# Depthwise convolution for two token tiles at once, as two half-rate streams with three short filters

## The chip, the cores and the metric

The kernel runs on one core of one Trainium2 chip. Its engines work side by side, each through its own queue of instructions in a fixed order: TensorE (PE in the profile; PEld is its weight load), VectorE (DVE), ScalarE (ACT), GpSimd (POOL) and SyncE (SP), which here only issues transfers. They meet through semaphores. Transfers are issued from the SP and ACT queues. The metric is the device time of one execution in microseconds; lower is better.

## The reference

One decoder layer in float32 on x of 2048 tokens by 1024 channels:

```
hn   = rms_norm(x);  proj = hn @ w_in                  # q, k, v and u (2 x 512 channels)
h    = a * sigmoid(gate)            # u = a, gate
h    = depthwise causal conv(h, width 31) + bias       # per channel, along the tokens
conv = silu(layer_norm(h over channels)) @ w_conv_pw
attn = sliding-window attention (window 128, sinks, relative bias)
h    = x + rms_norm(concat(attn, conv) @ w_out)
out  = h + rms_norm((silu(n @ w_gate) * (n @ w_up)) @ w_down),  n = rms_norm(h)
```

The part that changes is the depthwise convolution: y[n] is the sum over j from 0 to 30 of w[j] g[n - 30 + j], plus a bias, for 512 channels, each with its own 31 weights.

## The kernel before

The tokens are worked in four tiles of 512 (T), the channels in blocks of 128 partitions. Matmuls carry float32 as a high and a low part, three products for one (`three`). The stages, by the letter that the profile shows behind the @ of a tile's name:

- **A0 to A3** (`stage_a`): the input projections of one token tile, 14 units of 24 matmuls. The gated input of the convolution goes to DRAM, channel block by channel block (`glu`, stored in `glu_scr`, which sets `g{t}{c}` in `started`).
- **B0 to B3** (`stage_b`): attention, by blocks of 128 tokens. Its score bias lives in a tile of the tag `mb` until the last block.
- **C0 to C3**: the convolution, in two stages. `stage_taps(t)` loads one channel block with a halo of 30 tokens (`conv_in`, tag `glu`), makes the first product and then 30 multiply-and-add instructions on DVE, each over 512 tokens and each onto the accumulator y (tag `fc`), and stores y to `y_scr`. `stage_tail(t)` loads y again, turns it on TensorE, does the LayerNorm, the swish and the pointwise product, and stores the result to `mixT` (`conv_tail`). Its own work tiles have the tag `fc` too.
- **W0 to W3** (`stage_w`): the output projection of a token tile, which reads `mixT` (four attention blocks, then four blocks from the convolution), and its norm (`norm_w`).
- **H** (`stage_h_plain`, `stage_h_sums`), **F** and **G**: the channel mixer, for two pairs of token tiles, with seven products for eight. H turns the normed rows into operands; "S0" names the sums of operands for the first pair. F is the gate/up part: first plain products (`stage_pre`), then the sums with the other steps (`stage_p1`). G is the down part (`stage_p2`); in the first of them also the output projections of the second pair.

The order of work: the main line is a chain of `run(...)` calls; each of its steps moves a clock on by its cost. Beside it there are lanes (class `Lane`), lists of stages that give out work at a given rate per unit of that clock: `lc` the taps, `ld` the tails of tiles 0 and 1, `lw` the output projections, `lh` the operands, `lb` attention, and others. A stage in a lane can have a condition: W0 needs tail C0; C0 needs the taps T0 and ten units more; C3 likewise T3. From the code's emission order with priorities, a scheduler writes the fixed order of each queue. The taps are emitted with a priority 100 steps later than the main work (`LC`), and each is tied behind the last DVE instruction of the main work (`dve`). `BUFS` gives the number of buffers of each tag, which all tiles of this tag share.

The taps of tile 0 run during A0 and A1 and those of tile 1 behind them. During W1 and the first gate/up products the lane is held until S0 is done (`lc.hold`); tile 2's taps then go at a rate of 0.4 under the gate/up sums, tile 3's at 0.1 there and at 0.9 under the first down stage.

Of the kernel before, what the change touches and what calls it, by code (L numbers as in the profile page):

```python
# [12 lines left out]
F32 = mybir.dt.float32  # L13
F32R = mybir.dt.float32r
BF16 = mybir.dt.bfloat16
I8 = mybir.dt.int8
# [14 lines left out]
TAPS = 31  # L31
HALO = TAPS - 1
EPS = 1e-6
NEG = -1e30
# [3 lines left out]
def layer_kernel(ctx, tc, x, xT, cols, rows, sinks, relb, onehot, w_in, w_pw, w_out, w_gate, w_up, w_down, out):  # L38
# [13 lines left out]

    BUFS = dict(x=4, p=4, wx=1, gb=2, hl=8, ql=4, chl=5, mid=4, mb=2, fa=4, at=2, fc=3, glu=2, yt=1, raw=2, w=6)

# [6 lines left out]
    def f2(tag, shape=(P, T)):  # L61
        return t_(tag, shape)
# [161 lines left out]
    hn_scr = dr.tile([S, D], F32, name="hn_scr")  # L224
    y_scr = dr.tile([4, P, S], F32, name="y_scr")
    qs = {}
# [14 lines left out]
    def row_norms(ts, tag):  # L241
        lab[0] = f"A{ts[0]}"
        n = 4 * len(ts)
        ssq = sm(n)
        for i in range(n):
            xt = f4(tag)
            r0 = ts[0] * T + i * P
            nc.sync.dma_start(xt, x[r0 : r0 + P])
            act(junk, xt, AF.Square, accum_out=ssq[:, i : i + 1])
        r = rsqrt(ssq, n, D)  # L250
        for j, t in enumerate(ts):
            rn[t] = r[:, 4 * j : 4 * j + 4]
# [262 lines left out]

    def conv_in(t, c):
        g = t_("glu", (P, 576))[:, 0 : HALO + T]
        if t == 0:
            nc.vector.memset(g[:, 0:HALO], 0.0)
            nc.sync.dma_start(g[:, HALO:], glu_scr[c, :, 0:T])  # L520
        else:
            nc.sync.dma_start(g, glu_scr[c, :, t * T - HALO : (t + 1) * T])
        y = f2("fc")
        vts(y, g[:, 0:T], dwh[:, c, 0:1], dwb[:, c : c + 1], ALU.mult, ALU.add)
        return g, y

    def turner(yt, ycs):
# [7 lines left out]

    def stage_taps(t):
        L = f"C{t}"
        for c in range(4):
            while f"g{t}{c}" not in started:
                yield None  # L540
            lab[0] = L
            g, y = conv_in(t, c)
            for j in range(1, TAPS):
                stt(y, g[:, j : j + T], dwh[:, c, j : j + 1], y, ALU.mult, ALU.add)
                yield 0.68
                lab[0] = L
            nc.sync.dma_start(y_scr[c, :, t * T : (t + 1) * T], y)
            yield 0.68

    def stage_tail(t):  # L550
        L = f"C{t}"
        lab[0] = L
        yt = t_("yt", (P, 4, 4 * P))
        ycs = []
        turn = turner(yt, ycs)
        for c in range(4):
            lab[0] = L
            y = f2("fc")
            nc.sync.dma_start(y, y_scr[c, :, t * T : (t + 1) * T])
            ycs.append(y)  # L560
            turn(c)
            yield 0.5
        yield from conv_tail(t, yt)

    def conv_tail(t, yt):
# [30 lines left out]
        for m in range(4):  # L596
            raw = f2("fc")
            nc.sync.dma_start(raw, w_pw[m])
            w = split_w(raw, "mb" if t == 1 and m % 2 else "chl").rearrange("p a (k c) -> p a k c", c=P)
# [4 lines left out]
            nc.scalar.dma_start(mixT[4 + m, :, t * T : (t + 1) * T], z)  # L604
            yield 2
            lab[0] = L
# [102 lines left out]
    def norm_w(w, spill, acc, mtag):  # L709
# [4 lines left out]
        for s in range(4):  # L714
            act(junk, acc[s], AF.Square, accum_out=ssq[:, s : s + 1])
            yield 0.5
            lab[0] = L
# [4 lines left out]
        for s in range(4):  # L722
            lab[0] = L
            post_scale(acc[s], gb, r[:, s : s + 1])
            r0 = w * T + s * P
            if s == (2 if mtag == "fa" else 0):
                xt = f4("wx")
# [8 lines left out]
            nc.sync.dma_start(h_scr[r0 : r0 + P], acc[s])  # L736
            act(junk, acc[s], AF.Square, accum_out=ssq2[:, s : s + 1])
            yield 1.5
# [316 lines left out]
    def finish(L, gb, jobs, pool=True):  # L1055
# [3 lines left out]
        for j, (rows_, halves) in enumerate(jobs):  # L1059
            for n in range(2):  # L1060
                act(junk[:, 0:T], halves[n], AF.Square, scale=D**-0.5, accum_out=ssq[:, 2 * n + j : 2 * n + j + 1])
# [15 lines left out]
    def stage_p2(ws, am, td, last=False):  # L1077
# [60 lines left out]
        def scale_even(h):  # L1138
            for b in (2 * h, 2 * h + 1):
                lab[0] = L  # L1140
                c = home("c11", "x", b)
                act(junk[:, 0:T], c, AF.Square, scale=D**-0.5, accum_out=sse[:, b : b + 1])
                ptt(c, c, gbs[0], ALU.mult)
                yield 4.0

        def after(ty, b):
# [11 lines left out]
            elif ty == 3:  # L1158
                vtt(home("p7", "x", b), o, home("x2", "p", b), ALU.subtract)
                if b == 3:  # L1160
                    for n in range(2):
                        gbs.append(t_("glu", (P, 576))[:, 0:T])
                        nc.sync.dma_start(gbs[n], rows[1, n * T : (n + 1) * T].partition_broadcast(P))
# [48 lines left out]
        for b in range(4):  # L1212
# [3 lines left out]
            ssq = sm(1)  # L1216
            act(junk[:, 0:T], banks[b], AF.Square, scale=D**-0.5, accum_out=ssq)
            g = f2("fa")
# [59 lines left out]

    RC0, RC1, RC2, RC3, RW0, RW, RB, LC = 0.7, 1.1, 0.4, 0.9, 1.7, 1.25, 0.8, 100
    TAPS0 = 6  # L1280
# [6 lines left out]
    RT = 0.3  # L1287
    RP = 0.1
    NS = 12
# [171 lines left out]
```

## Time and profile before

| | us |
|---|---|
| median of 3 runs | 2048.06 |
| lowest and highest run | 2045.74, 2054.27 |
| profiled execution: span from first to last instruction | 2045.2 |
| TensorE busy | 1959.9 |
| DVE busy | 1499.2 |
| ACT busy | 984.4 |
| GpSimd busy | 408.5 |
| 480 tap instructions on DVE (the group's busy time) | 367.7 |

The profiled execution's own time is given as this span alone; no separate run time is listed for it, and the lowest run is 0.5 us above it. In a row that groups instructions one reads: line of the code, engine, operation, output tiles<-input tiles, shapes, xcount | busy us, mean ns of one | idle time of the engine before them and what ended it. DVE instructions issued through the helper `dve` all show its line, L85; they are told apart by tiles. A row of waits has: who waited <- for whom: us in total, times, longest. A row of a timeline has: start us, us, engine, line, operation, tiles, and in brackets the idle time before it and what ended it. A row of stages has the stretch, its length, and then the busy time and number of instructions of each engine in it.

### The profile page before, as it was taken

The page shows a single profiled execution, that of the slowest core. Times are in us where ns is not written, and L with a number is a line of the kernel's source. Part 1 is how long each engine was busy: PE and PEld are TensorE (multiplying, and loading weights), DVE is VectorE, ACT ScalarE, POOL GpSimd, SP SyncE. Part 2 cuts the span into 40 slices and gives each one's busy share as a digit, 9 for nine tenths or more (in the row PEclk, how much of TensorE's full clock was granted, in tenths as well). Part 3 has the DMA queues.
Part 4 walks back from the last instruction along what each step waited for, and adds up shares of the span by engine and source line. Part 5 has one row for each costly group of instructions (what it writes and reads, how often), then busy time and mean ns, then how long its engine had stood idle before and what let it go on. Part 6 is the DMA issues. An engine that isn't in the chain of part 4 may idle for free. (4 is left out here: it accounts for less than half of the span.)

```text
span 2045.2 us, 27190 instructions
## 1 busy us (share of the span) xinstructions
PE 1959.9 (96%) x8826; PEld 1565.3 (77%) x8826; DVE 1499.2 (73%) x2623; ACT 984.4 (48%) x1938; POOL 408.5 (20%) x466
## 2 busy tenths in 40 slices
PE   8999999999989999999989999999999999999997
PEld 6777767776667778778878878877788888888886
DVE  4999896995885899887749985577666665545557
ACT  5355455456546633334346457556643433345443
POOL 4011223333111300000001012115423333221003
PEclk9999999999999999999999999999999999999998
DMA  8787645578559876884486778678954453366654
GB/s 305 256 300 228 205 135 185 180 235 279 186 155 330 292 242 224 294 270 168 140 262 205 231 260 287 191 278 304 337 177 162 149 169 112 103 236 212 206 190 144
DMA packets 235902, 451.44 MB, mean 221 GB/s; under 512 B 23496, under 2 KB 49264, under 8 KB 235760
## 3 DMA queue, kind: packets, MB, share of 16 engines
q1 hardware_dynamic: 215216, 419.30, 62.6%
q10 hardware_dynamic: 20544, 30.42, 4.0%
q8 instruction: 69, 1.13, 0.2%
q14 instruction: 73, 0.60, 0.1%
HBM read 330.60 MB, written 119.02 MB: 220 GB/s over the span
## 5 line engine op out<-in xcount | busy, mean ns | idle before, releaser
L85 DVE SCALAR_TENSOR_TENSOR fc@C<-glu@C,colt,fc@C 128x512 f32<-128x512 f32 x480 | 367.7, 778 | 3.5
L846 PE MATMUL mm@F<-hl@H,w@F 128*128 128x512 f32 x1056 | 253.3, 390 | 2.5 <-ACT mm@F L886 1.5
L1116 PE MATMUL mm@G<-hl@G,hl@G 128*128 128x512 f32 x924 | 230.0, 398 | 8.2 <-DVE x@G L85 4.8
L846 PEld LDWEIGHTS mm@F<-hl@H,w@F 128*128 128x128 f32 x1056 | 197.6, 188 | 44.7 <-ACT mm@F L886 2.3
L170 PE MATMUL mm@A<-hl@A,w@A 128*128 128x512 f32 x840 | 207.3, 398 | 5.2 <-ACT w@A L110 1.4
L1116 PEld LDWEIGHTS mm@G<-hl@G,hl@G 128*128 128x128 f32 x924 | 174.6, 191 | 47.0 <-ACT hl@G L759 6.9
L1116 PE MATMUL mm@G<-w@G,hl@G 128*128 128x512 f32 x876 | 199.4, 389 | 0.0
L759 ACT ACTIVATE w@F<-chl@F 128x512 fp32r<-128x512 f32 x220 | 134.8, 624 | 130.9 <-PE mm@F L846 122.2
L1116 PEld LDWEIGHTS mm@G<-w@G,hl@G 128*128 128x128 f32 x876 | 164.4, 188 | 34.1
L170 PEld LDWEIGHTS mm@A<-hl@A,w@A 128*128 128x128 f32 x840 | 155.9, 189 | 42.2 <-ACT w@A L110 2.2
L85 DVE TENSOR_TENSOR w@F<-chl@F,w@F 128x512 fp32r<-128x512 f32 x198 | 145.4, 738 | 33.8 <-ACT w@F L759 33.4
L846 PE MATMUL mm@F<-ql@H,w@F 128*128 128x512 f32 x528 | 127.9, 391 | 11.0 <-ACT w@F L759 7.3
L846 PE MATMUL mm@F<-mid@H,w@F 128*128 128x512 f32 x528 | 130.4, 392 | 2.8 <-ACT mm@F L886 2.6
L846 PE MATMUL mm@F<-p@H,w@F 128*128 128x512 f32 x528 | 130.6, 393 | 0.0
L846 PE MATMUL mm@F<-x@H,w@F 128*128 128x512 f32 x528 | 127.4, 395 | 2.3 <-ACT fa@F L908 2.3
L846 PEld LDWEIGHTS mm@F<-ql@H,w@F 128*128 128x128 f32 x528 | 98.6, 188 | 33.7 <-ACT w@F L759 8.1
L846 PEld LDWEIGHTS mm@F<-x@H,w@F 128*128 128x128 f32 x528 | 99.8, 190 | 24.0 <-ACT fa@F L908 2.8
L846 PEld LDWEIGHTS mm@F<-mid@H,w@F 128*128 128x128 f32 x528 | 98.3, 188 | 26.0 <-ACT mm@F L886 4.6
L846 PEld LDWEIGHTS mm@F<-p@H,w@F 128*128 128x128 f32 x528 | 100.1, 190 | 21.3 <-ACT at@F L1007 0.4
L170 PE MATMUL mm@W<-w@W,hl@W 128*128 128x512 f32 x384 | 102.3, 411 | 7.7 <-ACT hl@W L681 6.8
L110 ACT ACTIVATE w@A<-raw@A 128x512 fp32r<-128x512 f32 x110 | 67.6, 627 | 82.7 <-PE mm@A L170 50.8
L476 POOL TENSOR_SCALAR_AFFINE_SELECT p@B<-p@B 128x512 f32<-128x512 f32 x62 | 59.1, 959 | 228.0 <-ACT p@B L474 226.3
(301 smaller groups left out, 3422.8 us busy)
## 6 DMA issues: line engine op xcount, KB each, us to landing
mids<-fa@F SPq DMA_DIRECT2D x154, 256.0 KB, 2.8
raw@A<-w_in SPq DMA_DIRECT2D x55, 512.0 KB, 4.5
w@A<-lo_in SPq DMA_DIRECT2D x84, 256.0 KB, 3.5
fc@G<-mids SPq DMA_DIRECT2D x77, 256.0 KB, 3.5
fa@G<-mids SPq DMA_DIRECT2D x75, 256.0 KB, 4.3
gb@F<-keeps SPq DMA_DIRECT2D x72, 256.0 KB, 4.3
raw@W<-w_out SPq DMA_DIRECT2D x32, 512.0 KB, 5.1
w@W<-lo_out SPq DMA_DIRECT2D x48, 256.0 KB, 3.9
```

The source lines that it names most:

```text
L85: r = op(*args, **kw)
L110: act(w[:, 0], raw, AF.Copy)
L170: mat(o, a, b, start=first and i == 0, stop=last and i == n - 1)
L476: nc.gpsimd.affine_select(out=pg[:, kb].rearrange("p (i q) -> p i q", q=P), in_=pg[:, 1].rearrange("p (i q) -> p i q", q=P), compare_op=AL ...
L759: act(w[:, 0], x, AF.Copy)
L846: mat(o, w[:, a, ks], op[k][:, b], start=first and n == 0, stop=n == 11, skip_group_check=not first)
L1116: mat(banks[b], p_, q_, start=start and z == 0, stop=stop and z == 2, skip_group_check=True)
```

## The change

The taps are done for two token tiles at a time, p = 0 for tiles 0 and 1 and p = 1 for tiles 2 and 3. Of the 1024 + 30 tokens of a channel block, e are the even and o the odd ones, 527 each (LE), read in place with a step of two elements. The filter is split into its even and odd weights, 16 and 15 (`dwe`, `dwo`), and a third filter of 16 weights, their sums (`dws`). Three short filters then give both output streams: a = even filter on e, b = odd filter on o (513 outputs), and the sum filter on x = e + o. The even outputs are a + b + bias, and the odd ones the sum filter's result less a and less b, moved on by one. The even outputs y and the odd ones a are stored separately (`y_scr` has an axis of two for them), so the tail works on a tile whose tokens are ordered 256 even, 256 odd; ScalarE puts them back in order when it writes the pointwise result.

```
-    BUFS = dict(... mb=2 ... fc=3, glu=2, yt=1, raw=2, w=6)
+    BUFS = dict(... mb=2 ... fc=3, glu=1, yt=1, raw=2, w=6)
...
+    dwe, dwo = dwh[:, :, 0::2], dwh[:, :, 1::2]
+    dws = cst.tile([P, 4, TAPS // 2 + 1], F32, name="dws")
+    nc.vector.tensor_copy(dws[:, :, 0:1], dwe[:, :, 0:1])
+    vtt(dws[:, :, 1:], dwe[:, :, 1:], dwo, ALU.add)
...
-    junk = cst.tile([P, D], BF16, name="junk")
+    junk = cst.tile([P, D], F8, name="junk")
...
-    def conv_in(t, c):
...
-    def stage_taps(t):
-        L = f"C{t}"
+    NE = TAPS // 2 + 1
+    LE = T + NE - 1
+    def stage_taps(p):
+        L = f"C{2 * p}"
         for c in range(4):
-            while f"g{t}{c}" not in started:
+            while f"g{2 * p + 1}{c}" not in started:
                 yield None
...
-            g, y = conv_in(t, c)
-            for j in range(1, TAPS):
-                stt(y, g[:, j : j + T], dwh[:, c, j : j + 1], y, ALU.mult, ALU.add)
-                yield 0.68
-            nc.sync.dma_start(y_scr[c, :, t * T : (t + 1) * T], y)
+            gt = t_("glu", (P, GW))[:, 0 : 2 * LE]
+            t0 = 2 * p * T
+            if p == 0:
+                nc.vector.memset(gt[:, 0:HALO], 0.0)
+                nc.sync.dma_start(gt[:, HALO:], glu_scr[c, :, 0 : 2 * T])
+            else:
+                nc.sync.dma_start(gt, glu_scr[c, :, t0 - HALO : t0 + 2 * T])
+            both = gt.rearrange("p (n two) -> p two n", two=2)
+            e, o = both[:, 0], both[:, 1]
+            bs = t_("wx", (P, GW))
+            b, x = bs[:, 0 : T + 1], bs[:, SOFF : SOFF + LE]
+            ay = t_("mb", (P, 2, T))
+            a, y = ay[:, 0], ay[:, 1]
+            vtt(x, e, o, ALU.add)
+            yield 0.68
+            vts(b, o[:, 0 : T + 1], dwo[:, c, 0:1], None, ALU.mult)
+            vts(a, e[:, 0:T], dwe[:, c, 0:1], None, ALU.mult)
+            yield 0.68
+            for j in range(1, NE):
+                if j < NE - 1:
+                    stt(b, o[:, j : j + T + 1], dwo[:, c, j : j + 1], b, ALU.mult, ALU.add)
+                    yield 0.68
+                stt(a, e[:, j : j + T], dwe[:, c, j : j + 1], a, ALU.mult, ALU.add)
+                yield 0.68
+            stt(y, a, dwb[:, c : c + 1], b[:, 0:T], ALU.add, ALU.add)
+            stt(a, a, dwb[:, c : c + 1], b[:, 1:], ALU.subtract, ALU.add)
+            nc.sync.dma_start(y_scr[c, :, p, 0], y)
+            yield 1.36
+            for j in range(NE):
+                stt(a, x[:, j : j + T], dws[:, c, j : j + 1], a, ALU.mult, ALU.add if j else ALU.subtract)
+                yield 0.68
+            nc.sync.dma_start(y_scr[c, :, p, 1], a)
+            yield 0.0
...
     def stage_tail(t):
-            nc.sync.dma_start(y, y_scr[c, :, t * T : (t + 1) * T])
+            h0 = (t % 2) * (T // 2)
+            nc.sync.dma_start(y.rearrange("p (two n) -> p two n", two=2), y_scr[c, :, t // 2, :, h0 : h0 + T // 2])
...
-            w = split_w(raw, "mb" if t == 1 and m % 2 else "chl")...
+            w = split_w(raw, "chl")...
...
-            act(z, o, AF.Copy, scale=0.5)
+            act(z.rearrange("p (n two) -> p two n", two=2), o.rearrange("p (two n) -> p two n", two=2), AF.Copy, scale=0.5)
...
     def norm_w(w, spill, acc, mtag):
-            if s == (2 if mtag == "fa" else 0):
+            if w > 1 and s == 0:
                 xt = f4("wx")
...
-    RC0, RC1, RC2, RC3, RW0, RW, RB, LC = 0.7, 1.1, 0.4, 0.9, 1.7, 1.25, 0.8, 100
+    RC0, RC1, RW0, RW, RB, LC = 1.1, 0.9, 1.7, 1.25, 0.8, 100
...
-    lc.rates = {"T0": RC0, "T1": RC1, "T2": RC2, "T3": RP}
+    lc.rates = {"T0": RC0, "T1": RC1}
...
-    for t in range(NT):
-        lc.add(f"T{t}", stage_taps(t))
+    for p in range(2):
+        lc.add(f"T{p}", stage_taps(p))
     for t in range(2):
-        ld.add(f"C{t}", stage_tail(t), lambda t=t: since(lc, f"T{t}", CS))
+        ld.add(f"C{t}", stage_tail(t), lambda: since(lc, "T0", CS))
...
-    lc.hold = lambda: "S0" not in lh.done
-    lh.add("S0", stage_h_sums(ws, ops), lambda: f"P0.{PRE_S0}" in started and "B3" in lb.done)
+    lh.add("S0", stage_h_sums(ws, ops), lambda: f"P0.{PRE_S0}" in started and "B3" in lb.done and "T1" in lc.done)
...
-    lc.until("T2")
-    lc.rates["T3"] = RC3
...
-    lw.add("C3", stage_tail(3), lambda: since(lc, "T3", CS))
+    lw.add("C3", stage_tail(3))
```

So in the changed kernel T0 and T1 name pairs. The taps of pair 0 begin when channel block 0 of tile 1 has been stored, those of pair 1 when that of tile 3 has. The tails C0 and C1 both wait for pair 0, S0 waits for pair 1, and no taps are left for the gate/up sums or the down stage. The accumulators move from `fc` to `mb` (y and a) and `wx` (b and x); for that, `norm_w` loads x in halves where W0 and W1 used `wx`, and the tail of tile 1 no longer uses `mb`. The tile into which ScalarE writes the squares, whose values nothing reads, is fp8 in place of bf16 (`saturate=False` at each use).

More of the change, by code (lines that the diff above doesn't have):

```diff
@@ L14 @@
 F32R = mybir.dt.float32r
-BF16 = mybir.dt.bfloat16
+F8 = mybir.dt.float8e4
 I8 = mybir.dt.int8
@@ L32 @@
 HALO = TAPS - 1
+GW = 1152
+SOFF = 544
 EPS = 1e-6
@@ L51, in nm @@
         return f"{s}@{lab[0]}_{uid[0]}"
-    BUFS = dict(x=4, p=4, wx=1, gb=2, hl=8, ql=4, chl=5, mid=4, mb=2, fa=4, at=2, fc=3, glu=2, yt=1, raw=2, w=6)
+    BUFS = dict(x=4, p=4, wx=1, gb=2, hl=8, ql=4, chl=5, mid=4, mb=2, fa=4, at=2, fc=3, glu=1, yt=1, raw=2, w=6)
     def t_(tag, shape, dt=F32):
@@ L224, in layer_kernel @@
     hn_scr = dr.tile([S, D], F32, name="hn_scr")
-    y_scr = dr.tile([4, P, S], F32, name="y_scr")
+    y_scr = dr.tile([4, P, 2, 2, T], F32, name="y_scr")
     qs = {}
@@ L514, in stage_b @@
                 yield from back(b - 1)
-    def conv_in(t, c):
[L517 to L525, printed above, removed]
     def turner(yt, ycs):
@@ L598, in conv_tail @@
             nc.sync.dma_start(raw, w_pw[m])
-            w = split_w(raw, "mb" if t == 1 and m % 2 else "chl").rearrange("p a (k c) -> p a k c", c=P)
+            w = split_w(raw, "chl").rearrange("p a (k c) -> p a k c", c=P)
             o = ct()
@@ L602, in conv_tail @@
             z = f2("gb" if t > 1 else "fc")
-            act(z, o, AF.Copy, scale=0.5)
+            act(
+                z.rearrange("p (n two) -> p two n", two=2),
+                o.rearrange("p (two n) -> p two n", two=2),
+                AF.Copy,
+                scale=0.5,
+            )
             nc.scalar.dma_start(mixT[4 + m, :, t * T : (t + 1) * T], z)
@@ L714, in norm_w @@
         for s in range(4):
-            act(junk, acc[s], AF.Square, accum_out=ssq[:, s : s + 1])
+            act(junk, acc[s], AF.Square, saturate=False, accum_out=ssq[:, s : s + 1])
             yield 0.5
@@ L1060, in finish @@
             for n in range(2):
-                act(junk[:, 0:T], halves[n], AF.Square, scale=D**-0.5, accum_out=ssq[:, 2 * n + j : 2 * n + j + 1])
+                act(junk[:, 0:T], halves[n], AF.Square, scale=D**-0.5, saturate=False, accum_out=ssq[:, 2 * n + j : 2 * n + j + 1])
                 (ptt if pool or n else vtt)(halves[n], halves[n], gb[n], ALU.mult)
@@ L1160, in after @@
                 if b == 3:
+                    gbt = t_("glu", (P, GW))
                     for n in range(2):
-                        gbs.append(t_("glu", (P, 576))[:, 0:T])
+                        gbs.append(gbt[:, n * T : (n + 1) * T])
                         nc.sync.dma_start(gbs[n], rows[1, n * T : (n + 1) * T].partition_broadcast(P))
@@ L1287, in layer_kernel @@
     RT = 0.3
-    RP = 0.1
     NS = 12
```

13 lines of the change are left out of this document (9 added, 4 removed).

## The prediction

> **What bounds the kernel now.** I read the page's totals first, then the busy time by stage, then TensorE's waits, and last the timeline of the queues around the convolution.
>
> ```profile
> span 2045.2 us, 27190 instructions
> PE 1959.9 (96%) x8826; PEld 1565.3 (77%) x8826; DVE 1499.2 (73%) x2623; ACT 984.4 (48%) x1938; POOL 408.5 (20%) x466
> L85 DVE SCALAR_TENSOR_TENSOR fc@C<-glu@C,colt,fc@C 128x512 f32<-128x512 f32 x480 | 367.7, 778 | 3.5
> ```
>
> TensorE is busy 1959.9 of 2045.2 us. The change adds no matmul and removes none, so all that it can win is idle time of TensorE, 85.3 us in all. By stage (columns: stretch, its length, then PE, PEld, DVE, ACT and POOL busy with their instruction counts, clock, DMA share, GB/s):
>
> ```profile
> 0.00:126.00 126.00, 119.74 (x537) 94.69 (x538) 98.19 (x199) 62.04 (x116) 27.00 (x43) 0.99 0.87 301
> 126.00:310.00 184.00, 180.07 (x897) 134.95 (x896) 165.96 (x372) 93.62 (x236) 38.26 (x50) 1.00 0.63 194
> 310.00:486.00 176.00, 166.34 (x782) 123.30 (x781) 145.03 (x284) 88.55 (x208) 67.57 (x82) 0.97 0.65 208
> 486.00:543.00 57.00, 52.09 (x261) 36.89 (x261) 32.93 (x92) 37.56 (x87) 9.78 (x9) 1.00 0.73 246
> 543.00:678.00 135.00, 121.81 (x549) 93.59 (x546) 102.21 (x185) 73.95 (x152) 25.22 (x42) 0.96 0.73 243
> 678.00:709.00 31.00, 30.71 (x138) 25.09 (x137) 26.51 (x37) 20.22 (x38) 9.65 (x7) 1.00 0.82 277
> 709.00:1035.00 326.00, 312.64 (x1360) 254.69 (x1359) 262.86 (x422) 120.30 (x216) 0.00 (x0) 0.99 0.68 225
> 1035.00:1325.00 290.00, 279.86 (x1246) 229.15 (x1245) 215.90 (x345) 158.32 (x278) 42.91 (x66) 0.99 0.74 240
> 1325.00:1480.00 155.00, 144.54 (x642) 116.74 (x642) 110.33 (x186) 94.91 (x184) 61.54 (x62) 0.98 0.88 302
> 1480.00:1828.00 348.00, 347.69 (x1534) 287.31 (x1533) 210.28 (x277) 136.58 (x242) 96.96 (x69) 1.00 0.47 157
> ```
>
> TensorE idles 6.3 us up to 126, 3.9, 9.7, 4.9, 13.2 and 0.3 us in the next five stretches (projections, W0, W1, first gate/up products), 13.4 us in the gate/up sums of the first pair (709 to 1035), 10.1 and 10.5 us in the first down stage and the passage to the second pair, 0.3 us in the second pair's sums. These last do the same work as those of 709 to 1035, without a convolution and with part of the subtractions on GpSimd: DVE 60% against 81%.
>
> Where the taps lie now (DVE, instructions that read the glu tiles, same stretches):
>
> ```profile
> 126.00:310.00 184.00, 98.08 (x129) 1.00 0.63 194
> 310.00:486.00 176.00, 71.57 (x93) 0.97 0.65 208
> 486.00:543.00 57.00, 4.72 (x7) 1.00 0.73 246
> 543.00:678.00 135.00, 40.07 (x53) 0.96 0.73 243
> 678.00:709.00 31.00, 2.78 (x4) 1.00 0.82 277
> 709.00:1035.00 326.00, 50.82 (x69) 0.99 0.68 225
> 1035.00:1325.00 290.00, 65.23 (x84) 0.99 0.74 240
> ```
>
> **The size of a tap.** One lasts 778 ns in the mean, but neighbours overlap:
>
> ```profile
> 351.87 3.39 DVE L85 SCALAR_TENSOR_TENSOR fc@C<-glu@C,colt,fc@C 128x512 f32<-128x512 f32 x5
> 324.13 0.55 DVE L85 TENSOR_SCALAR fc@C<-glu@C,colt 128x512 f32<-128x512 f32 x1 [6.50 <-DMA mixT<-fc@C]
> ```
>
> Five in 3.39 us: four pitches of 0.66 and one length of 0.74, an overlap of 0.08. So one tap takes 0.66 (undisturbed) to 0.78 us from the engine; I use 0.70, the mean less the overlap. The old code needs 31 per channel and tile, 496. The new one needs per channel and pair 1 sum, 2 first products, 14 + 15 taps, 2 joins and 16 taps: 50, so 400 in all. DVE saves 96 x 0.70 = 67 us, but it isn't the bound; only place counts.
>
> Of the 50, 32 read every second element. No row here shows such an operand. Lower bound: nothing; upper: twice the pitch, 256 x 0.66 = 169 us. I take nothing, since 512 results are written either way and the nearest row is the same instruction. The Trainium skill, SBUF — State Buffer, section "Door 1: The DMA port swizzle", says that two hits per 16-byte line keep full rate; two fp32 words of such a line are used here, so by it 400 passes cost 280 us and by the other bound 449 us. No run so far shows it.
>
> **Does it fit?** The first pair can start when channel 0 of tile 1 is in (stored at 118.87, about 126 after landing and load); the second pair must be out of the `mb` tiles before the sums stage writes there, at 678.7:
>
> ```profile
> 118.87 0.32 SPq L338 DMA_DIRECT2D glu_scr<-fa@A  x1
> L832 ACT ACTIVATE mb@H<-chl@H x4: 614/628/632, 678.7 to 1477.4; 128x512 fp32r<-128x512 f32 x4
> 230.42 0.32 SPq L547 DMA_DIRECT2D y_scr<-fc@C  x1
> 294.92 0.34 ACTq L604 DMA_DIRECT2D mixT<-fc@C  x1
> 331.34 0.33 ACTq L604 DMA_DIRECT2D mixT<-fc@C  x1
> 368.52 0.90 SPq L679 DMA_DIRECT2D fa@W<-mixT  x2
> 401.49 0.86 SPq L679 DMA_DIRECT2D fa@W<-mixT  x2
> 543.36 0.98 PE L846 MATMUL mm@F<-x@H,w@F 128*128 128x512 f32 x3
> 518.04 1.40 DVE L85 TENSOR_TENSOR x@H<-gb@H,x@H 128x512 fp32r<-128x512 f32 x1 [3.06 <-ACT x@H L800]
> ```
>
> Room for taps is length less the rest of DVE's work (busy less taps, plus 0.08 per tap): 106, 95, 28, 69 us in the first four stretches, 298 us to 678. Needed: 280 at 0.70, so 94% full. Pair 0 (140 us) ends 34 us of room into the third row's stretch, at 310 + 34/0.54 = 373; pair 1 takes the remaining 61, then 28, and ends about 643. That is 35 us early. `lc.hold`, which kept taps back until S0, goes, and in its place S0 waits for "T1"; behind S0 in its lane stands nothing, but the first gate/up sums need its operands. Price nothing, ends 0 and +26 (below).
>
> **W0 waits longer.** Now tile 0's taps end at 230.42, and its pointwise results go out 64.5 to 101 us later; W0 fetches them at 368.52 and 401.49. With 373 they go out at 438 to 474, 69 to 73 us after those fetches. Behind W0's sums stand its norm, the turned operands (the last `x` operand at 518.04 + 1.40) and the first gate/up product at 543.36, a slack of 24 us; so at most 48 us later. Against it: the tail's `fc` tiles, which the accumulators shared (row 324.13: a tap waits 6.5 us for a tail's store), are now the tail's alone; W1's second half (96 matmuls of 0.24, 23 us), which came after the first products, can come ahead, since tile 1's tail is no longer behind tile 0's by a tap stage; matmuls of A3 fill until 486. I take +6, ends -5 and +25.
>
> **What 709 to 1480 wins.**
>
> ```profile
> PE mm@F L846 <- ACT w@F L759: 7.3, 2, 4.4
> ACT mm@F L993 <- DMA gb@F<-keeps: 74.0, 18, 10.2
> SPq L1027 <- DVE fa@F L85: 36.8, 25, 5.5
> SPq L935 <- DVE w@F L85: 24.3, 17, 5.6
> PE tr@W L170 <- ACT mid@W L652: 5.1, 1, 5.1
> PE mm@G L1116 <- DVE x@G L85: 4.8, 1, 4.8
> PE ct@C L531 <- DMA fc@C<-y_scr: 3.0, 1, 3.0
> ```
>
> In the sums SP waits for DVE, the kept blocks queued behind it land late, ACT waits for them and TensorE for ACT. Taps give back 69 x 0.70 = 48 of DVE's 263 us (81% to 66%). I take 9 of the 13.4 us idle, not all, since the weight sums and their transfers stay; ends 0 and 13. The down stage loses 84 taps: the 3.0 us wait for tile 3's last row goes, and part of the rest; 5 of 10.1, ends 0 and 8 (what is late next is the `mid` tile of the 5.1 us row, which no tap holds). W3 no longer waits for tile 3's taps, so its norm runs further ahead of the passage: 5 of 10.5, ends 0 and 8.
>
> **Small parts, taken as nothing.** `glu` has one buffer: the next load (8 instead of 16, on SP between weight loads) waits for the last half-rate tap, and 18 passes, 12 us, lie between that and its use. `mb` has one free slot while the score bias lives: a new accumulator waits for the last store, some 4 us, but 15 taps of the odd stream need not; uncovered, 7 x 4 = 28 us of DVE's room. The tail reads y in two pieces of 1 KB; ScalarE writes z with a gap (16 x 0.6 us, doubled at worst, 2.4 us on W0's path); W0 and W1 add x in halves (one more DMA each, under 1 us); the second pointwise weights of tile 1 have one slot, as tile 0's have now; the small DVE work for the summed filter falls in the start; the fp8 scrap tile is as long as the bf16 one.
>
> **Sum.** +6 - 9 - 5 - 5 = -13: 2045.2 becomes 2032.2. The median of the runs, 2048.06, stands 2.9 above this execution's span; so 2035 for the median. About 0.5%, 10 us, is what a measurement of this kernel can tell from no change.
>
> **Rivals.**
> Hidden anyway: the idle of 709 to 1480 belongs to transfers and bank turns, not to taps. For it: DMA share 0.68 to 0.88 there; the 5.1 us row names no tap. Against: SP waiting for DVE 36.8 and 24.3 us. It keeps -19 at about -5, with W0's +6: 2049, a tie.
>
> Too full (slower): DVE becomes the bound until 709. Its price is set by the tap: above 298/400 = 0.745 us the second pair runs past 678. At 0.76 it needs 304, the last 6 us at 7 us of room per 31: end 704, the sums stage and the first products that need it 26 us late; 2048 + 6 + 26 - 19 = 2061. At 0.78 it needs 311 against 305 to 709, the rest at a third of the time: 727, 48 us late and 2083. For it: 778 ns mean, 0.77 per tap in 310 to 486 (71.57/93) where GpSimd is busy 68 us, against 0.74 (50.82/69) in 709 to 1035 where it has nothing; 153 passes leave quiet places. Against: that is only 4%, and DVE was busy 166 of the 184 us from 126 to 310 while TensorE idled 3.9. The Trainium skill, GPSIMD Engine Reference, section "1. Specifications", says that GpSimd's SBUF interfaces are shared with DVE instructions that have two SBUF inputs, as every tap has; the trace's 0.77 against 0.74 agrees, and by that rule this rival is the likelier, by no stated figure.
>
> Half rate costs double: 280 + 169 = 449 us against 305: 144 us left at 709, a third of the time free: some hundreds late, at least 2150.
>
> **Chances.** Forecast 0.47, hidden 0.24, too full 0.26, double 0.03. So faster 0.47, same 0.24, slower 0.29. The likeliest alone: 2022 to 2038, by the ends of its terms. To hold 8 in 10 the range takes in the tie and the too-full case up to about 0.765 per tap: 2020 to 2068.
>
> **What would show it.** Right: 50 passes per channel and pair at about 0.75 us each; last y store of pair 0 near 373, of pair 1 before 678; first gate/up product by about 550; DVE near 95% from 126 to 640; idle TensorE in 709 to 1035 near 4 us. Wrong: strided passes longer than the contiguous ones; the first gate/up product after 570; TensorE waiting for the sums stage near 711; TensorE's idle after 709 still above 30 us.

## The result, and the profile after

The changed kernel takes 2112.4 us (2107.25 to 2121.55) where the kernel before, run beside it, took 2049.2: a ratio of 1.032 (1.028 to 1.035). It is slower by 63 us. The forecast was 2035, with 2020 to 2068 as its range.

The page after (the totals; share of the span, then instructions):

```profile
span 2105.5 us, 27138 instructions
PE 1980.8 (94%) x8826; PEld 1578.7 (75%) x8826; DVE 1448.8 (69%) x2530; ACT 990.4 (47%) x1938; POOL 410.7 (20%) x467
```

VectorE (DVE) did get lighter, by 50 us (67 were forecast). TensorE's idle time rose from 85.3 to 124.7 us, and the same 8826 matmuls also took 20.9 us longer. Together that is the 60.3 us by which the two profiled executions differ. Busy time by stage, cut at the same events as the table of before (projections to 310, end of A3's matmuls, first gate/up product, S0's first `mb` tile, first sums products, first down matmul, and then the later stretches, each 60 us on):

```profile
core 0: us, PE busy (x) PEld busy (x) DVE busy (x) ACT busy (x) POOL busy (x), PEclk, DMA share, GB/s
310.00:513.00 203.00, 170.14 (x762) 124.47 (x761) 167.83 (x310) 88.85 (x197) 68.37 (x83) 0.90 0.51 165
513.00:588.00 75.00, 62.57 (x260) 43.53 (x259) 59.73 (x127) 45.94 (x101) 20.96 (x24) 0.82 0.66 227
588.00:739.00 151.00, 126.27 (x569) 97.53 (x568) 133.35 (x235) 77.23 (x157) 32.39 (x42) 0.94 0.74 245
739.00:775.00 36.00, 30.06 (x124) 23.36 (x123) 28.33 (x42) 18.87 (x34) 8.80 (x6) 0.95 1.00 351
775.00:1095.00 320.00, 312.89 (x1361) 256.71 (x1360) 213.81 (x338) 120.98 (x215) 0.00 (x0) 0.99 0.60 205
1095.00:1385.00 290.00, 278.75 (x1245) 227.57 (x1243) 158.32 (x272) 160.05 (x282) 43.29 (x67) 0.99 0.72 235
1385.00:1540.00 155.00, 146.03 (x634) 116.76 (x634) 106.16 (x170) 91.44 (x177) 55.58 (x58) 0.97 0.86 297
```

The first four rows hold 32.9, 12.4, 24.7 and 5.9 us of idle TensorE, where before had 9.7, 4.9, 13.2 and 0.3, and their granted clock is 0.82 to 0.95 where it was 0.96 to 1.00. All of the loss lies here. The last three rows, for which the change was meant, idle 7.1, 11.3 and 9.0 us (before 13.4, 10.1 and 10.5): a gain of some 7 us.

The rows that carry the path from the taps to the sums, after (stores and loads of the queues: start, length; groups: count, shortest/median/longest in ns, first and last start):

```profile
361.53 0.32 SPq L583 DMA_DIRECT2D y_scr<-mb@C  x1
433.92 0.34 ACTq L646 DMA_DIRECT2D mixT<-fc@C  x1
462.71 0.33 ACTq L646 DMA_DIRECT2D mixT<-fc@C  x1
436.36 0.32 SPq L721 DMA_DIRECT2D fa@W<-mixT  x1
467.28 0.70 SPq L721 DMA_DIRECT2D fa@W<-mixT  x1
L87 DVE TENSOR_TENSOR x@W<-x@W,mm@W x24: 649/680/689, 361.5 to 490.1; 128x512 f32<-128x512 f32 x24
L888 PE MATMUL mm@F<-x@H,w@F x528: 387/389/793, 587.7 to 1880.1; 128*128 128x512 f32 x176
717.89 0.33 SPq L583 DMA_DIRECT2D y_scr<-mb@C  x1
L874 ACT ACTIVATE mb@H<-chl@H x4: 619/626/631, 738.7 to 1542.6; 128x512 fp32r<-128x512 f32 x4
```

and W0's weight sums before:

```profile
L85 DVE TENSOR_TENSOR x@W<-x@W,mm@W x24: 672/675/683, 361.9 to 438.8; 128x512 f32<-128x512 f32 x24
```

Pair 0's last y is stored at 361.5, C0's results go out at 433.9 to 462.7, W0 fetches them at 436.4 to 467.3 (before: 368.5 to 401.5), its last weight sum stands at 490.1 (438.8), the first gate/up product at 587.7 (543.4), and S0's first `mb` tile at 738.7 (678.7). The product is late by 44 us, the landmarks from S0 on by 59 to 65, and the end by 60.

### The profile page after: what moved, and what is told of

The parts are those of the page before. It is cut to its first block, busy times and chain, and to the rows that moved or that the text cites. A ratio compares the mean times of both kernels' runs of the same rounds, so it can differ in the third digit from the quotient of the medians.

```text
span 2105.5 us, 27138 instructions
## 1 busy us (share of the span) xinstructions
PE 1980.8 (94%) x8826; PEld 1578.7 (75%) x8826; DVE 1448.8 (69%) x2530; ACT 990.4 (47%) x1938; POOL 410.7 (20%) x467
## 5 line engine op out<-in xcount | busy, mean ns | idle before, releaser
L888 PE MATMUL mm@F<-hl@H,w@F 128*128 128x512 f32 x1056 | 257.8, 395 | 9.4 <-ACT mm@F L928 9.4
L172 PE MATMUL mm@W<-w@W,hl@W 128*128 128x512 f32 x384 | 103.9, 418 | 10.6 <-ACT x@W L694 4.9
L87 DVE SCALAR_TENSOR_TENSOR mb@C<-wx@C,dws,mb@C 128x512 f32<-128x512 f32 x128 | 106.2, 830 | 1.8
L172 PE MATMUL tr@W<-w@W,ql@W 128*128 128x512 f32 x384 | 99.4, 397 | 6.7 <-ACT mid@W L694 4.8
```

Of the source, the lines that this page charges most:

```text
L87: r = op(*args, **kw)
L172: mat(o, a, b, start=first and i == 0, stop=last and i == n - 1)
L888: mat(o, w[:, a, ks], op[k][:, b], start=first and n == 0, stop=n == 11, skip_group_check=not first)
```

## The experiments

Three landmarks turned out to describe every run: W0's first gate/up product, S0's first `mb` tile, and the time. The marks are those of each kernel's profiled execution, the time is the median of its runs. The time less the S0 mark is 1365 to 1377 us in all thirteen kernels (1365 to 1373 within the profiled executions), so what moves S0 moves the end.

| kernel | first gate/up product | S0's first mb tile | time (median) |
|---|---|---|---|
| before | 543.4 | 678.7 | 2049.2 to 2053.7 |
| after | 587.7 | 738.7 | 2112.4 |
| first pair only | 590.9 | 723.2 | 2100.2 |
| second pair only | 569.4 | 722.8 | 2099.0 |
| loads in gb | 592.6 | 745.1 | 2115.2 |
| x halves in at | 595.4 | 750.9 | 2116.4 |
| A3 first | 589.0 | 742.1 | 2115.0 |
| W0 does not wait for C0 | 557.5 | 723.4 | 2095.0 |
| second pair only, its taps cut | 559.2 | 692.4 | 2063.9 |
| all taps cut | 545.9 | 678.4 | 2047.9 |
| no wait for C0, pair 1's taps cut | 553.2 | 691.8 | 2061.1 |
| no wait for C0, pair 1's taps earlier | 555.8 | 712.8 | 2082.1 |
| pair 1's taps earlier | 596.6 | 734.3 | 2104.0 |

My first theory, from the profile after, was one of buffers. No projection matmul of A3 runs between 400 and 440, while TensorE idles 16 of these 40 us. W0's four loads of the convolution's blocks stand in the order ahead of A3's gates and hold the four `fa` buffers until C0's results come, and half-used weights hold `w`. Its rivals were that DVE has too much to do (the forecast's "too full"), and that C0's lateness alone sets the first gate/up product.

**One pair at a time.** The kernel after, with only one of the pairs in the new form; the other two tiles have 31 passes each, as before. With the first pair new, tiles 2 and 3 are again held back until S0, as before (the hold begins behind W1 in the order of work, not with it, so that 97 of their 248 passes ran ahead of S0 here, and 91 in the kernel before):

```diff
-    for p in range(2):
-        lc.add(f"T{p}", stage_taps(p))
+    lc.add("T0", stage_taps(0))
+    for t in (2, 3):
+        lc.add(f"T{t}", stage_taps_old(t))
...
+    lc.hold = lambda: "S0" not in lh.done
```

and with the second:

```diff
-    for p in range(2):
-        lc.add(f"T{p}", stage_taps(p))
+    for t in (0, 1):
+        lc.add(f"U{t}", stage_taps_old(t))
+    lc.add("T1", stage_taps(1))
```

> The kernel after, but only the first pair of tiles (0 and 1) in half-rate form; tiles 2 and 3 as before, with 31 passes each and held back until S0. Theory (slots: the first pair's late C0 makes W0's waiting loads hold the fa and w buffers that A3 needs, so TensorE starves at 400 to 450): nearly all of the loss stays, first gate/up product at about 585, total 2090 to 2110. Rival (too full: DVE cannot do 400 passes before the gate/up sums): with half of them back behind S0 the loss goes, first gate/up product near 545 to 555, total 2045 to 2060.

> The kernel after, but only the second pair (tiles 2 and 3) in half-rate form, done ahead of the gate/up sums; tiles 0 and 1 one after the other as before. Theory (slots): TensorE is no longer starved at 400 to 440, the first gate/up product stands near 543 as before, S0's mb tiles are written near 685 and the total is 2035 to 2060. Rival (too full): the first gate/up product is near 543 too, but S0's mb tiles come near 740 and the total stays at 2080 or above.

Measured: 1.023 (1.020 to 1.026) and 1.024 (1.020 to 1.027), so each half of the change costs about as much as three quarters of the whole. The first pair alone moves the first gate/up product by 47 us and what follows by no more. With most of pair 1's work back behind S0, DVE was idle for more than half of the time just where TensorE starved:

```profile
400.00:440.00 40.00, 18.46 (x70) 10.23 (x70) 15.48 (x47) 18.16 (x40) 14.87 (x26) 0.67 0.25 78
440.00:480.00 40.00, 36.06 (x148) 27.36 (x148) 8.04 (x13) 12.15 (x21) 8.95 (x7) 0.95 0.52 166
```

(columns as in the table of stages: DVE is busy 15.48 of 40 us and 8.04 of 40.) So a full DVE isn't the cause at the front. The second pair alone missed what my theory said of it: the first gate/up product was 26 us late, though C0 was done in good time, and S0 another 18. Two causes, then, and they do not add up: each pair alone puts S0 44 us later, both together 60.

**Other buffers.** W0's convolution blocks in `gb` in place of `fa`; and, in a second kernel, W1's first two halves of x in `at` in place of `fa`:

```diff
-                m = f2(mtag)
+                m = f2("gb" if w == 0 and c >= 4 else mtag)
```

```diff
-                    xt = f2(mtag if s == 1 or w > 1 else "fa")
+                    xt = f2(mtag if s == 1 or w > 1 or w == 1 and s == 0 else "fa")
```

> The kernel after, with one change: W0's loads of the convolution's four blocks take gb buffers instead of fa. Theory (slots): A3's gate tanh is no longer kept from its fa buffer, projection matmuls run at 400 to 440 (at least 5 us of them, after has none), A3's last one comes 10 to 25 us earlier than at 513, total 10 to 25 us less than after (2087 to 2102). Rival (chain: C0's lateness alone sets the first gate/up product, what TensorE does meanwhile doesn't matter): projection matmuls move, the first gate/up product and the total stay within 5 us of 588 and of 2112. Rival (too full): the same, and S0 stays at 739.

> The kernel after, with one change: the two x halves that W1 loads first take the at buffers instead of fa. Theory (the halves of x hold two fa buffers, and ScalarE's fa@F behind them makes TensorE wait 9.8 us at 675): that wait falls to about 2 us and the total by about 7 us (2103 to 2107). Rival (the wait is C1's lateness, whichever buffer the halves take): the wait stays at 6 to 10 us and the total within 3 us of 2112.

Measured: 1.031 (1.028 to 1.034) and 1.031 (1.027 to 1.036), against 1.032 of the kernel after: no change. With `gb`, A3 still had no matmul between 400 and 440. With `at`, the wait at 675 stayed (at 685 there). After, and then with `at` (TensorE's waits from 590 to 800: in total, times, longest):

```profile
PE mm@F L888 <- ACT fa@F L950: 9.8, 1, 9.8
```

```profile
PE mm@F L888 <- ACT fa@F L950: 8.7, 1, 8.7
```

So neither of these buffers was the cause, and the row's 9.8 us wasn't a cost of the halves of x; both expectations of mine failed.

**A3 first.** W0's convolution blocks, and all that follows them, come into the order only when A3's unit 10 stands there. (The blocks are fetched two at a time, and the wait stands ahead of the first two; the expectation below speaks of the last two.)

```diff
         def step(u):
+            started.add(f"A{t}.{u}")
...
+                while w == 0 and (gi, n) == (1, 1) and "A3.10" not in started:
+                    yield None
                 lab[0] = L
                 if n == 1 and gi + 1 < KC // G and not (ready and G * gi + G == 4):
                     nxt = acts(gi + 1)
```

> The kernel after, with one change: W0's loads of the last two convolution blocks, and all that follows them, are put into the order of the work only once A3's unit 10 stands in it. Theory (order: W0's waiting loads and the w and fa buffers that they hold keep A3's matmuls away from 400 to 440): A3 has at least 8 us of matmuls there, TensorE's idle time between 400 and 440 falls from 16 to under 6 us, first gate/up product at 565 to 578, total 2090 to 2103. Rival (chain: C0's lateness alone sets the first gate/up product): A3 comes earlier, the first gate/up product stays at 583 to 595 and the total within 5 us of 2112.

Measured: 1.031 (1.028 to 1.033). Busy time from 400 to 580, after:

```profile
400.00:440.00 40.00, 24.24 (x83) 13.63 (x83) 38.23 (x65) 19.11 (x42) 17.23 (x16) 0.63 0.34 106
480.00:540.00 60.00, 59.33 (x256) 44.59 (x254) 50.40 (x95) 38.22 (x65) 26.09 (x45) 0.91 0.69 237
540.00:580.00 40.00, 28.24 (x118) 20.36 (x120) 24.84 (x56) 26.02 (x66) 8.29 (x7) 0.79 0.66 227
```

and with A3 first:

```profile
400.00:440.00 40.00, 35.94 (x184) 25.84 (x183) 29.62 (x54) 25.62 (x58) 22.23 (x19) 1.00 0.59 169
480.00:540.00 60.00, 30.83 (x140) 22.47 (x138) 42.38 (x91) 38.30 (x77) 20.06 (x43) 0.77 0.62 218
540.00:580.00 40.00, 31.89 (x134) 22.93 (x135) 22.78 (x42) 21.59 (x50) 10.78 (x9) 0.75 0.59 192
```

The hole at 400 to 440 closes (18.8 us of A3's matmuls are there now) and opens again at 480 to 540, where TensorE idles 29 us. The first gate/up product stays at 589. Two things cancel in that: C0's last result came 9 us later than after (471.7 for 462.7), and the passage from W0's last weight sum to the product took 7 us less. So the starved matmuls were a symptom; to give A3 this time did not bring the product forward. My theory of buffers and order falls, and the rival of the chain stands.

**C0's lateness taken away.** W0 fetches attention blocks again in place of the convolution's, in the same places:

```diff
-                nc.sync.dma_start(m, mixT[c, :, w * T : (w + 1) * T])
+                nc.sync.dma_start(m, mixT[c - 4 if w == 0 and c >= 4 else c, :, w * T : (w + 1) * T])
```

> The kernel after, except that W0 fetches attention blocks a second time in place of its four convolution blocks, in the same places of the order, so that it never waits for C0; every load, matmul and tap is still there. Left out: the convolution's part of the first projection tile (its sums come out of the attention blocks twice). Theory (the late C0 costs the 44 us at the front, by way of W0's waiting loads): first gate/up product at 545 to 560, S0's mb tiles at 700 to 715, total 2070 to 2085; what is left is the second pair's taps on DVE. Rival (the taps on DVE delay the small operations of everything else): first gate/up product at 575 or later, total above 2095.

Measured: 1.022 (1.020 to 1.024). The first gate/up product came 30 us earlier, so most of its 44 us are C0's lateness. Yet the time fell by 17.5 us only, less than expected, since S0 moved by just 15: something else than the product held S0 by then.

**The taps cut.** To see whether that is pair 1's taps, 41 of the 50 passes per channel were left out, with the order unchanged: in the kernel with the second pair alone (there only pair 1 has the new form, so that `j < 2` decides), and in both pairs of the kernel after:

```diff
-                    stt(b, o[:, j : j + T + 1], dwo[:, c, j : j + 1], b, ALU.mult, ALU.add)
+                    if p == 0 or j < 2: stt(b, o[:, j : j + T + 1], dwo[:, c, j : j + 1], b, ALU.mult, ALU.add)
...
-                stt(a, e[:, j : j + T], dwe[:, c, j : j + 1], a, ALU.mult, ALU.add)
+                if p == 0 or j < 2: stt(a, e[:, j : j + T], dwe[:, c, j : j + 1], a, ALU.mult, ALU.add)
...
-                stt(a, x[:, j : j + T], dws[:, c, j : j + 1], a, ALU.mult, ALU.add if j else ALU.subtract)
+                if p == 0 or j < 2: stt(a, x[:, j : j + T], dws[:, c, j : j + 1], a, ALU.mult, ALU.add if j else ALU.subtract)
```

(for both pairs the condition is `j < 2` alone).

> The experiment with only the second pair in half-rate form, with 9 of the 50 passes per channel of that pair issued; everything else, the planner's order too, is the same. Left out: 41 of 50 passes of tiles 2 and 3, so their convolution is wrong. Theory (the +26 at the first gate/up product and the +18 up to S0 are the second pair's taps on DVE): first gate/up product at 540 to 550, S0's mb tiles at 675 to 690, total 2035 to 2055. Rival (the small parts: x in halves, the tail's pieces, the order without a hold): first gate/up product at 560 or later, total 2080 or above.

> The kernel after, with 9 of the 50 passes per channel issued in both pairs, in the same places of the order. Left out: 41 of 50 passes, so the convolution is wrong. C0 is then early and DVE has 230 us less to do. Theory (lateness of C0 and taps on DVE are all of the loss): first gate/up product at 530 to 545, S0's mb tiles at 665 to 685, total 2025 to 2050. Rival (small parts and order carry a share of the loss): total 2065 or above.

Measured: 1.006 (1.003 to 1.009) and 0.998 (0.996 to 1.000). Pair 1's taps cost 35 of the 47 to 49 us of the second pair alone. The remaining 13 us lie outside my expectation. The first gate/up product is 16 us late there too: W0's normed rows are stored 6 us later than before (497.3 for 491.1), and their turning behind that takes 10 us more. Why it does, the runs don't settle. With all taps cut the loss is gone, landmark by landmark:

```profile
L888 PE MATMUL mm@F<-x@H,w@F x528: 387/389/628, 545.9 to 1825.4; 128*128 128x512 f32 x176
L874 ACT ACTIVATE mb@H<-chl@H x4: 621/628/632, 678.4 to 1486.0; 128x512 fp32r<-128x512 f32 x4
719.00:1037.00 318.00, 309.93 (x1356) 254.24 (x1355) 211.82 (x335) 119.67 (x213) 0.00 (x0) 0.99 0.61 206
```

So up to S0 the small parts cost nothing that shows. From S0's first tile to the first product with it, though, it takes 40.2 us (678.4 to 718.6) where before took 32.6, and the sums behind are shorter by about as much; what those 7.6 us are is not shown. This run also gives, for this order of the work, the upper bound that I should have asked for first. With hardly any convolution on DVE, the whole kernel gains 2.5 us (0.2%). Its gate/up sums (third row) idle 8.1 us, no less than the 7.1 of the kernel after; they and the two stretches behind them idle 26.5 us in all, 27.3 after and 34.0 before. So at most some 7 us of that idle time belonged to the taps; there were never 19 us to win.

**Two paths.** First both causes are taken away together (W0 fetches attention blocks, pair 1's taps are cut, pair 0's 200 passes stay). Then W0 fetches attention blocks and pair 1's taps are only put into the order faster; and last the complete kernel with that rate:

```diff
-    RC0, RC1, RW0, RW, RB, LC = 1.1, 0.9, 1.7, 1.25, 0.8, 100
+    RC0, RC1, RW0, RW, RB, LC = 1.1, 1.4, 1.7, 1.25, 0.8, 100
```

> Two of the causes taken away together: W0 fetches attention blocks in place of the convolution's (it never waits for C0), and of pair 1's taps only 9 of 50 passes per channel are issued; pair 0's 200 passes stay. Left out: the convolution's part of the first projection tile and 41 of 50 passes of tiles 2 and 3. Theory (two separate paths to S0, each with its own price: C0's lateness at the front, pair 1's taps on DVE behind it): first gate/up product at 540 to 552, S0's mb tiles at 680 to 695, total 2045 to 2065, as with nearly all taps gone. Rival (the first pair's taps, which fill DVE from 200 to 360, delay the other work by themselves): S0 at 705 or later, total above 2075.

> W0 fetches attention blocks in place of the convolution's, and pair 1's taps are put into the order half as fast again (the planner's rate 1.4 for 0.9). Left out: the convolution's part of the first projection tile. Against the same without the faster rate (2095, S0's mb tiles at 723, pair 1's last store at 702). Theory order (DVE idles 54 us between 361 and 718 there with taps still to do, since they stand behind other work in its order): pair 1's last store at 640 to 675, S0 at 695 to 712, total 2065 to 2085. Rival capacity (DVE has no room, faster taps only delay the other work): the first gate/up product moves from 557 to 565 or later, S0 within 8 us of 723, total 2090 or above.

> The kernel after, complete, with pair 1's taps put into the order half as fast again (the planner's rate 1.4 for 0.9). Theory (two paths to S0, and the later one counts: the first pair's late C0 holds the first gate/up product at 585 to 595, and the work between that product and S0 takes 132 us or more, as with the first pair alone in the new form): S0's mb tiles at 720 to 735, total 2096 to 2110, a small gain at most. Rival (pair 1's taps alone decide the end): a gain of 13 us, as where W0 did not wait for C0, total 2099 or less with S0 at 712 to 722.

Measured: 1.005 (1.004 to 1.007), 1.017 (1.013 to 1.021) and 1.025 (1.022 to 1.029). Without both causes 10 us remain of 63, so the first pair's taps, which fill DVE from 200 to 360, cost no more than that by themselves. With only the rate changed (and no wait for C0), pair 1's last store comes 42 us earlier, S0 10.6 us and the end 13 us. In the complete kernel S0 gains 4 us and the time 8 us: the first gate/up product came 9 us later (596.6), and what stands behind it in the order came later with it. (Four of the marks of these runs and of the one with all taps cut fell 0.8 to 1.6 us outside what was expected: 545.9, 553.2, 712.8 and 596.6.) Without a wait for C0, pair 1's last store at the planner's old rate, and the same and S0's mark at the new one:

```profile
702.50 0.38 SPq L583 DMA_DIRECT2D y_scr<-mb@C  x1
```

```profile
660.52 1.13 SPq L583 DMA_DIRECT2D y_scr<-mb@C  x1
L874 ACT ACTIVATE mb@H<-chl@H x4: 621/627/633, 712.8 to 1513.7; 128x512 fp32r<-128x512 f32 x4
```

DVE was busy 303.3 us of 361 to 718 in the one and 313.6 in the other: it had had room, and the order of its queue left it unused. But the order isn't all, as S0 followed pair 1's store by 21 us in the one and by 52 in the other.

**What S0 needs besides.** S0 turns the normed rows of W1 (`hn_scr`, which `norm_w` stores), and W1's second half needs C1's results. In all thirteen kernels S0's first `mb` tile follows the last store of these rows by 32 to 42 us, so S0 moves with these rows. W1's last fetch and last stored row, before and then after:

```profile
593.74 0.33 SPq L679 DMA_DIRECT2D at@W<-mixT  x1
647.12 1.00 ACTq L747 DMA_DIRECT2D hn_scr<-mid@W  x1
```

```profile
634.32 0.37 SPq L721 DMA_DIRECT2D at@W<-mixT  x1
699.92 0.33 ACTq L789 DMA_DIRECT2D hn_scr<-mid@W  x1
```

Without a wait for C0, C1's last result and the same two, at the planner's old rate and then at the new one:

```profile
615.84 0.33 ACTq L646 DMA_DIRECT2D mixT<-fc@C  x1
618.98 0.33 SPq L721 DMA_DIRECT2D at@W<-mixT  x1
685.61 0.33 ACTq L789 DMA_DIRECT2D hn_scr<-mid@W  x1
```

```profile
614.53 0.33 ACTq L646 DMA_DIRECT2D mixT<-fc@C  x1
618.37 0.33 SPq L721 DMA_DIRECT2D at@W<-mixT  x1
675.77 0.34 ACTq L789 DMA_DIRECT2D hn_scr<-mid@W  x1
```

In the kernel after, W1's last fetch stands 41 us later than before, behind the late gate/up products, which the order puts ahead of W1's second half. Where W0 does not wait, that fetch follows C1's last result by 3 to 4 us instead (before, C1 was done at 536.3). So C1's lateness is a third path, and it explains why pair 1's taps, stored 42 us earlier, moved S0 by 10.6 us only: W1's last fetch came 0.6 us earlier and the rows 9.8. With pair 1's taps cut as well, the fetch is still 11 us late (604.8), right behind C1's last result at 600.9; the 10 us that remain there are most likely this. No run takes C1's lateness away alone.

No version here beats the kernel before. The bound by the run with all taps cut, 2.5 us, says that none with fewer passes in these places of the order would by more than a measurement can tell.

## Why the prediction was wrong

**The taps: right on the stride, too low on the size.** 50 passes per channel and pair were forecast at 0.70 us from the engine and nothing extra for every second element. After, the rows of the contiguous stream and of the two strided ones (shortest/median/longest, ns), and the same groups with busy us and mean ns:

```profile
L87 DVE SCALAR_TENSOR_TENSOR mb@C<-wx@C,dws,mb@C x128: 735/752/1834, 155.7 to 717.1; 128x512 f32<-128x512 f32 x128
L87 DVE SCALAR_TENSOR_TENSOR mb@C<-glu@C,colt,mb@C x120: 733/742/1831, 126.0 to 671.2; 128x512 f32<-128x512 f32 x120
L87 DVE SCALAR_TENSOR_TENSOR wx@C<-glu@C,colt,wx@C x112: 695/745/1782, 125.3 to 691.6; 128x513 f32<-128x513 f32 x112
L87 DVE SCALAR_TENSOR_TENSOR mb@C<-wx@C,dws,mb@C 128x512 f32<-128x512 f32 x128 | 106.2, 830 | 1.8
L87 DVE SCALAR_TENSOR_TENSOR mb@C<-glu@C,colt,mb@C 128x512 f32<-128x512 f32 x120 | 96.6, 805 | 0.2
L87 DVE SCALAR_TENSOR_TENSOR wx@C<-glu@C,colt,wx@C 128x513 f32<-128x513 f32 x112 | 92.5, 826 | 0.6
```

The medians are 742 and 745 ns strided and 752 contiguous: no price for the stride. By the Trainium skill's rule (SBUF — State Buffer, "Door 1: The DMA port swizzle") two hits per 16-byte line keep full rate, and the trace agrees. The rival "half rate costs double" is out. The means, though, are 805 to 830 ns where before had 778. By the prediction's own working (mean less 0.08 of overlap) a pass took 0.74 us and not 0.70, and 400 of them need 296 us of the 298 that it counted as room. That is the edge of "too full", which began at 0.745.

**Pair 0 and C0: right.** The last store was forecast at 373 and came at 361.5. C0's results were forecast at 438 to 474 and came at 434 to 463.

**"W0 waits longer": the step that failed most.** The mechanism was right. Its own bound, "at most 48 us later", was near the answer, 44.3. I took +6, with ends of −5 and +25, for three reliefs. The runs show what they were worth. The tail did not get faster with the `fc` tiles to itself: C0's results went out 72 to 101 us behind the last store, and 64.5 to 101 before. That A3's matmuls fill the time until 486 is no relief for a chain of latencies: A3 first left the product at 589. And W1's second half did not come ahead: its 96 matmuls stand behind the first gate/up product as they did before. That the bound came so near is in part luck, since it counted on 24 us of slack between the last `x` operand and the product, and 19 of these were still there after (568.7 to 587.7). What was won lies elsewhere: W0's last fetch was 66 us later and its last sum 51, and from that sum to the product it takes 104.6 us before (438.8 to 543.4) and 97.6 after (490.1 to 587.7). With A3 first this passage took 90.5, which is the least that any run shows.

**"S0 not late": failed.** The term was 0, with ends of 0 and +26; from the first gate/up product to S0 it took 151 us for 135, so +16. Pair 1's last store stood at 717.9, not 643. Part of this is the size of a pass: pair 1's 200 passes took 155 us of DVE (each from its start to the next instruction's, or to its own end) where 140 were forecast. The larger error lies in "room for taps is length less the rest of DVE's work". Between 361 and 718 DVE was busy 292.5 us and idle 64.5 (29 of them in 440 to 500), with taps still to be done: pair 1's second channel block had been loaded at 407.6. They stood in its queue behind work that waited for others. The largest of these waits from 440 to 500, after (in total, times, longest):

```profile
DVE hl@W L87 <- ACT hl@W L723: 12.8, 3, 5.8
```

The prediction also let the taps hold S0 by their end alone. The way by which they did most of it is W1's norm: from W1's last sum to its last normed row it took 49.5 us after (650.4 to 699.9), 37.1 before, and 37 to 38 in the three kernels with pair 1's taps cut. From that row to S0 it took 7 us more than before. The rival "too full" had the place right and half of the reason: the passes did grow, to the edge of its condition, but most of the delay is room that could not be used.

**"What 709 to 1480 wins": failed in size.** P1 −9, first down stage −5, passage −5, in all −19. Measured from the idle times: −6.3, +1.2 and −1.5, some −7 in all. With nearly all taps cut these stretches idle hardly less. "Hidden anyway", which I gave 0.24, was right on this term: most of the idle time does not belong to the taps. That it belongs to transfers and bank turns is not shown. My evidence against that rival, SP waiting for DVE 36.8 and 24.3 us in the sums, says nothing about the taps: without them these two waits are 40.9 and 40.3 us.

**Small parts: right up to S0.** "Under 1 us" for x in halves, and the rest at nothing: with all taps cut, S0 stands at 678.4 as before. The 7.6 us between S0 and the first product with it, in that run, stay open. The 9.8 us wait at 675, which the profile after puts down to the halves' buffer, stayed when the buffer was changed.

The terms as measured: +44.3 at the first gate/up product, +15.7 from there to S0, +5.2 to the first sums products, −5.9 in the sums, +1.0 behind them; in all the 60.3 us between the two profiled executions. The range of the likeliest case, 2022 to 2038, is not the sum of its terms' ends; these add up to 2014 and, with S0's, to 2099, which the measured time still exceeds. The two pairs are not independent prices. The first pair alone puts S0 44.5 us later, the second alone 44.1, both 60.0: each hides part of the other, which is why undoing one half wins only 12 to 13 us of 63.

## What to carry to other kernels

Bound a change before you sum it: run, or work out, the kernel with the work removed altogether, since an engine that is 80% busy beside a full TensorE may have nothing to give. When work moves ahead, follow the chain behind its last result to the first product that needs it and count only slack that the latencies leave; other matmuls that could run meanwhile do not shorten it. Do it for each result that moves: here C0, C1 and pair 1's taps each had a way to S0, and taking one away showed the next. And idle time of an in-order engine is room only for work that its queue puts there; check the order, not the sum.

## What the runs showed of the hardware

Where TensorE starved, its clock fell too. In 400 to 440 it was busy 24.2 of 40 us and was granted 0.63 of its clock; with A3 in the same place it was busy 35.9 us, with 101 matmuls more, at 1.00. In all, the same 8826 matmuls took 1980.8 us of TensorE after and 1959.9 before. The longest 128x512 matmul of the gate/up row above took 793 ns against a median of 389, about twice. The Trainium skill, TensorE: Matmul & The Clock Gate, Part 1, says that the clock has two rates, half and full, set by how busy the array has lately been; the 793 against 389 agrees. These 20.9 us are not a third of the loss, though: with all taps cut the same matmuls took 1972.3 us, 12.4 more than before, and the kernel was as fast as before. Where TensorE would wait anyway, slow matmuls fill time that it had.

A multiply-and-add on DVE lasts longer when GpSimd works beside it. Of the 360 passes in the three groups after, the 262 during which no GpSimd instruction ran took 744 ns in the mean and at most 758; the other 98 took 1024, and all 49 passes above 900 ns are among them. Before, the same division gives 394 passes of 744 ns and 86 of 937. So a pass alone did not change, strided or not. Its mean grew because in the new places more of the passes fell beside GpSimd's work (27% for 18%) and were longer there, and the median hides that. (The profile's spans of GpSimd are rough, but no long pass stands outside them.)
